# Gathering the tokens of four experts at a time, ahead of a hinted branch

## The chip, the cores and the metric

The kernel runs on one core of one Trainium2 chip. The metric is the device time of one execution, in microseconds (us); lower is better. All inputs and weights are float32.

## The reference, cut to what matters

Two transformer blocks follow each other over 256 tokens of 1024 features. The first one ends in a mixture of 16 experts. The router gives each token two experts and a weight for each. Every expert is a gated product of width 512:

```
gates = jnp.sum(jax.nn.one_hot(idx, N_EXPERTS, dtype=f32) * w[..., None], axis=1).astype(h.dtype)
out = jnp.zeros_like(ht)
for e in range(N_EXPERTS):
    hid = jax.nn.silu(ht @ w_gate[e]) * (ht @ w_up[e])
    out = out + gates[:, e:e + 1] * (hid @ w_down[e])
```

Since an expert's gate is zero for most tokens, the kernel brings only the tokens that an expert was chosen for into that expert's up to 64 places, and adds the results back to the tokens they belong to. If some expert has more than 64 tokens, a branch runs every expert over every token instead.

## The kernel before, in words

Before and after the experts the work is a stream of large products on TensorE (PE). Weights arrive by DMA from the queue of SyncE (SP) in blocks of 1 MB, in a fixed order, into a ring of buffers; a block is asked for as soon as PE has let go of an older one (`load`, line 501). VectorE (DVE) and ScalarE (ACT) move results out of PSUM. The order on every engine is the order in which the program is written down. PSUM has eight banks; four of them (`pa`) hold the experts' sum throughout, so four are left to turn over.

The experts' part goes like this, in the lines that the change touches:

- The routing (lines 1575 to 1623) makes `mask` (256 tokens by 16 experts, 0 or 1) and, by a small product on PE, `rank`, the place that a token has within each expert. The same product gives the fullest expert's count, `most`.
- `gather(g)` (line 1628) serves a pair of experts. DVE builds `dp`, a 0/1 matrix that has a one where a token stands in a place: four instructions, one for each tile of 128 tokens and each of two experts, 64 places each. PE multiplies the tokens' features by it, both halves of their float32 (`h2H`, `h2L`): for each half of the features (`kq`) sixteen matmuls with 128 columns, into one PSUM bank, which DVE copies to `xg`. Then PE turns `dp` round (`back`, the way back) and picks the gates (`gsl`).
- Of the first pair the first half is gathered ahead of the branch (`next(first)`, lines 1661 and 1678) and the second half inside the first expert (lines 1841 to 1843). The other seven pairs are gathered as side work between the products of the experts (`side.add`, `side.tick`, `side.finish`, lines 1836 to 1851).
- Each engine reads the count `most_i` into a register (line 1681) and compares (line 1682, `tc.If`). The block under it is long: it holds every expert over every token. It is jumped over in the runs here.
- `gate_up` (line 1738) multiplies an expert's places by a block of weights, two matmuls of 512 columns beside each other on the array; `hidden` turns the result, `down` (line 1762) multiplies a pair's hidden values by the second weights, `combine` (line 1787) adds them to `pa` through `back`.

Names in rows: `raw` is a block of weights, `ps` a PSUM bank, `y` the result of `down`. L379 is the helper that records all instructions of PE, DVE and ACT; L515 and L512 issue the weights (L512 those that come in two half blocks).

The pair's gather before:

```
for m in range(2):
    for a in range(2):
        e = 2 * g + a
        V.tensor_scalar(dp[:, m, a], C("slots"), rank[:, m, e:e + 1], mask[:, m, e:e + 1], op0=OP.is_equal, op1=OP.mult)
```

Of the kernel before, what the change touches and what calls it, by code (L numbers as in the profile page):

```python
# [9 lines left out]
F32 = mybir.dt.float32  # L10
F32R = mybir.dt.float32r
I32 = mybir.dt.int32
# [13 lines left out]
# ----------------------------------------------------------------------------  # L26
# Constants that depend on shapes alone
# ----------------------------------------------------------------------------
# [14 lines left out]
def shape_constants():  # L43
# [19 lines left out]
    one["slots"] = np.tile(np.arange(64)[None, :] / 16, (128, 1))  # L63
# [3 lines left out]
    # axial rotary tables over a head's columns ordered (even | odd)  # L67
# [7 lines left out]
    # forward transform over 512 points of 256 samples: real parts of bins 0..255, imaginary  # L75
    # parts of bins 1..255 with bin 256 (real) in the place of the imaginary part of bin 0
# [12 lines left out]
    # positional features of the filters  # L89
# [7 lines left out]
    # inverse frequencies of the second block's rotary embeddings  # L97
# [3 lines left out]
    # log of the number of dilated windows that hold a key, as an additive mask  # L101
# [21 lines left out]
# ----------------------------------------------------------------------------  # L123
# Layout of the inputs
# ----------------------------------------------------------------------------


def pack(w, kt, cols):
    """[K, M] -> blocks [128, kt, cols], columns outermost, then the rows' groups."""
    k, m = w.shape  # L130
    v = w.reshape(k // (128 * kt), kt, 128, m // cols, cols)
    return np.ascontiguousarray(v.transpose(3, 0, 2, 1, 4)).reshape(-1, 128, kt * cols)


def feat(v):
    """[n*128] -> [128, n]"""
    return np.ascontiguousarray(v.reshape(-1, 128).T)


def lay_out(I):  # L140
    """The inputs as the kernel reads them: moved, never changed."""
# [43 lines left out]
    # per-feature parameters, a feature per partition  # L185
# [13 lines left out]
    # small weights of the filters' network and the decay, rows on partitions  # L199
# [40 lines left out]
# ----------------------------------------------------------------------------  # L240
# Order in which the weights stream in
# ----------------------------------------------------------------------------


# queries and keys (0) and values (1) of two heads each
# [3 lines left out]
def stream_order():  # L249
    """Blocks as (name, number, groups of 128 rows, columns, cut): a block that is split into halves of  # L250
    float32 is split in pieces: two by rows' groups ("k") or by columns ("c"), three ("3"), or one ("")."""
# [69 lines left out]
# ----------------------------------------------------------------------------  # L321
# The program
# ----------------------------------------------------------------------------
# [9 lines left out]
# where the blocks of the second modulation come: branch, block of its gate or of its product  # L333
# [3 lines left out]
# quarters of a product whose operands are not split  # L337
# [3 lines left out]
class Clocked:  # L341
    """An engine whose instructions are put on a rough timeline while they are written down, so that side work
    can be told to go on when what its next products need is about to be there."""
# [39 lines left out]
class Side:  # L383
    """Work that goes on between the products of the main stream: job after job, or two beside each other."""
# [4 lines left out]
    def add(self, gen, beside=None):  # L389
        """A job that waits for the ones before it, but for the one that it goes beside."""  # L390
        self.jobs.append([gen, max(Clocked.now["S"], Clocked.now["V"]) + 0.15, beside])
        return gen

    def next(self):
        """The job that is ready first."""
        a = self.jobs[:2]
        return a[1] if len(a) > 1 and a[1][2] is a[0][0] and a[1][1] < a[0][1] else a[0]
# [12 lines left out]
    def tick(self):  # L410
        """The next job's next step, if it needn't wait."""
# [8 lines left out]
def program(ctx, tc, A, out, dump=None):  # L420
# [24 lines left out]
    def T2(shape, name):  # L445
        """Tiles for the two halves of a float32 operand, in one place if they are small."""
# [20 lines left out]
    def bcast(ap, cols):  # L467
        """A [1, cols] row in DRAM, read by every partition."""
        return bass.AP(tensor=ap.tensor, offset=ap.offset, ap=[[0, 128], [1, cols]])

    def rsqrt(v, n, tag="us"):
        """1/sqrt(v) of a [128, n] tile: a first guess from the exponent, then Newton's steps."""
# [9 lines left out]
    def rsqrt1(v, eps, n=1, between=()):  # L482
        """1/sqrt(v / n + eps) of a [128, 1] tile, the same way; other work goes between the steps."""
# [35 lines left out]
    def ahead_of(name, b):  # L519
        """How many pieces are split ahead."""  # L520
# [95 lines left out]
    def lin_feat(wh, wl, j, x, ps):  # L616
        """Features on partitions: 128 columns of the weights stay, the tokens move."""
# [6 lines left out]
    def feat_block(name, b, x, per=1):  # L624
        """A block whose pieces hold `per` groups of 128 columns: pairs of groups, a bank each."""
# [69 lines left out]
    def sin_of(dst, src, n, parts):  # L695
        """sin of any float: the argument is brought near zero first."""
# [11 lines left out]
    def hy_filters():  # L708
# [54 lines left out]
        # the spectra of the odd and the even parts, without the division by the filters' sums  # L763
# [16 lines left out]
        # the sums: a channel per partition they divide what the convolution is multiplied with, and as  # L780
        # a row they multiply the direct path that is added to the even part's first sample
# [18 lines left out]
        for o in range(2):  # L800
# [3 lines left out]
            # bin 0 has no imaginary part: bin 256 in its place  # L804
# [5 lines left out]
    # silu(c) and silu(c_ctx) in the first two of 32 columns: a product's four parts of 512 outputs  # L810
    # lie on the array's four groups of columns
# [64 lines left out]
    def modulated(s):  # L876
        """The halves of the modulated features, two groups of 128 at a time."""
# [1466 lines left out]
```

## Time and profile before

| | |
|---|---|
| time, median of 3 runs | 1444.52 us (1441.32 to 1444.76) |
| span of the profiled execution | 1439.4 us |
| PE busy | 1382.4 us, 96% of the span |
| DVE busy | 846.3 us, 59% |
| ACT busy | 629.9 us, 44% |
| TensorE clock granted, mean | 0.989 |
| moved by DMA | 297.47 MB, mean 207 GB/s |

The profiled execution has its span from the first to the last instruction; its own time is not listed beside it, but the three runs lie 1.9 to 5.4 us above the span, the median 5.1 us above. A busy engine here is one with an instruction in flight. Matmuls overlap, so PE's pace is read from the starts of successive instructions, not from the duration of one.

### The profile page before, as it was taken

How to read it: one execution, taken by the hardware profiler on the slowest of the kernel's cores; microseconds unless marked ns; L12 is line 12 of the kernel's file. 1: busy time of each engine (PE TensorE's matmuls, PEld its weight loads, DVE VectorE, ACT ScalarE, POOL GpSimd, SP SyncE). 2: the span in 40 equal slices, each digit the busy share in tenths (PEclk: the TensorE clock that was granted, in tenths of full speed). 3: DMA queues.
4: the chain of work that ended last, by engine and by line, in shares of the span. 5: the costliest groups of instructions: out<-in, count | busy, mean ns of one | idle time of the engine just before them, and what ended most of it. 6: DMA issues, size and time to landing. Idle time of an engine off the chain costs nothing.

```text
span 1439.4 us, 20751 instructions
## 1 busy us (share of the span) xinstructions
PE 1382.4 (96%) x8462; PEld 1079.5 (75%) x8462; DVE 846.3 (59%) x1555; ACT 629.9 (44%) x1012; POOL 5.8 (0%) x13
## 2 busy tenths in 40 slices
PE   6999999999999699999999899999999998999998
PEld 2678899778796344444378679999977887999996
DVE  4777457455876421121166577666585888666675
ACT  5543465644343211111147646444445664545551
POOL 0000000000000000000000000000000000000000
PEclk9999999999999899999999999999999999999999
DMA  9523444546379799999643235555444453555540
GB/s 372 211 73 114 147 175 161 209 147 229 123 247 368 282 365 391 420 421 420 240 183 118 88 107 198 194 191 211 161 162 154 145 177 125 179 202 176 207 145 30
DMA packets 44629, 297.47 MB, mean 207 GB/s; under 512 B 5186, under 2 KB 6386, under 8 KB 10288
## 3 DMA queue, kind: packets, MB, share of 16 engines
q1 hardware_dynamic: 42012, 291.02, 54.3%
q10 hardware_dynamic: 1924, 3.27, 0.7%
q0 software_dynamic: 592, 1.79, 0.5%
q8 instruction: 69, 1.13, 0.3%
q14 instruction: 32, 0.26, 0.1%
HBM read 295.00 MB, written 1.05 MB: 206 GB/s over the span
## 4 chain that ended last, share of the span: by engine, by line
PE 57%; DVE 5%; ACT 2%; DMA 1%; issue 1%; ACTq 0%; SPq 0%; DVEq 0%
PE ps L379 47%; PE pd L379 7%; DVE w L379 2%; PE pa L379 1%; PE pq L379 1%; ACT pe L379 1%; DVE v L379 1%; DMA raw<-in_ab_q 1%; DVE sm L379 1%; ACT w L379 0%; DVE rs L379 0%; PE oc L379 0%; DVE xL L379 0%; DVE rsa L379 0%; DMA pt<-in_p 0%
## 5 line engine op out<-in xcount | busy, mean ns | idle before, releaser
L379 DVE TENSOR_TENSOR w<-raw,w 128x1024 fp32r<-128x1024 f32 (+3 forms) x301 | 346.4, 1194 | 84.9 <-ACT w L379 83.8
L379 ACT ACTIVATE w<-raw 128x1024 fp32r<-128x1024 f32 (+3 forms) x301 | 293.5, 1033 | 11.1 <-DVE w L379 4.8
L379 PE MATMUL ps<-xH,w 128*128 128x256 f32 x1408 | 256.5, 283 | 0.6 <-ACT xH L379 0.6
L379 PEld LDWEIGHTS ps<-xH,w 128*128 128x128 f32 x1408 | 220.6, 192 | 1.8 <-ACT xH L379 1.1
L379 PE MATMUL ps<-xL,w 128*128 128x256 f32 x704 | 199.3, 283 | 0.7 <-DVE xL L379 0.7
L379 PE MATMUL ps<-w,xH 128*128 128x512 f32 (+2 forms) x544 | 151.3, 364 | 4.0 <-ACT xH L379 2.1
L379 PEld LDWEIGHTS ps<-xL,w 128*128 128x128 f32 x704 | 134.9, 192 | 1.8 <-DVE xL L379 1.1
L379 PE MATMUL ps<-raw,xg 128*64 128x512 f32 x512 | 121.7, 608 | 8.2 <-DVEq L1682 8.0
L379 PE MATMUL pd<-w,fh 128*128 128x512 f32 x528 | 125.6, 394 | 0.0
L379 PE MATMUL ps<-hH,w 128*128 128x256 f32 (+1 forms) x608 | 115.7, 287 | 0.0
L379 PEld LDWEIGHTS pd<-w,fh 128*128 128x128 f32 x528 | 98.3, 189 | 21.6
L379 PEld LDWEIGHTS ps<-w,xH 128*128 128x128 f32 x544 | 95.9, 190 | 19.6 <-ACT xH L379 4.0
L379 PEld LDWEIGHTS ps<-hH,w 128*128 128x128 f32 (+1 forms) x608 | 94.9, 187 | 7.9 <-issue 2.7
L379 PE MATMUL ps<-w,xL 128*128 128x512 f32 (+2 forms) x272 | 98.5, 362 | 1.9 <-DVE xL L379 1.8
L379 PE MATMUL ps<-w,hH 128*128 128x512 f32 (+1 forms) x288 | 88.1, 390 | 0.0
L379 PE MATMUL ps<-hL,w 128*128 128x256 f32 (+1 forms) x304 | 85.9, 282 | 0.0
L379 PEld LDWEIGHTS ps<-raw,xg 128*64 128x64 f32 x512 | 34.2, 139 | 66.3 <-issue 57.0
L379 DVE SCALAR_TENSOR_TENSOR fc<-ps,par,fc 128x255 f32<-128x255 f32 x88 | 42.4, 482 | 51.6 <-ACT fc L379 50.0
L379 ACT ACTIVATE fc<-ps,par 128x256 f32<-128x256 f32 x44 | 24.8, 564 | 92.3 <-PE ps L379 66.4
L379 PEld LDWEIGHTS ps<-w,hH 128*128 128x128 f32 x288 | 52.2, 188 | 13.8 <-issue 2.7
L379 PEld LDWEIGHTS ps<-w,xL 128*128 128x128 f32 x272 | 51.6, 190 | 12.0 <-DVE xL L379 5.0
L379 PE MATMUL ps<-raw,hid 128*64 128x512 f32 x256 | 57.7, 595 | 0.0
(443 smaller groups left out, 1888.5 us busy)
## 6 DMA issues: line engine op xcount, KB each, us to landing
raw<-in_moe_gu SPq DMA_DIRECT2D x62, 1024.0 KB, 9.0
raw<-in_moe_down SPq DMA_DIRECT2D x32, 1024.0 KB, 10.3
raw<-in_mod SPq DMA_DIRECT2D x24, 1024.0 KB, 4.9
raw<-in_ffn_gate SPq DMA_DIRECT2D x22, 1024.0 KB, 4.7
raw<-in_ffn_up SPq DMA_DIRECT2D x22, 1024.0 KB, 4.8
raw<-in_ffn_down SPq DMA_DIRECT2D x22, 1024.0 KB, 4.7
raw<-in_w_brg SPq DMA_DIRECT2D x12, 1024.0 KB, 5.7
raw<-in_ple_gate SPq DMA_DIRECT2D x8, 1024.0 KB, 4.7
```

The source lines that it names most:

```text
L379: return f(*args, **kw)
```

## The change

The gather now serves four experts. `dp` has the places of four (256 columns) and is built by one DVE instruction: `rank` is made one larger where a token is chosen and zero elsewhere (in one instruction that replaces the copy of `rank`), the table of places is one larger too, and a plain comparison replaces the comparison and multiplication. The matmuls have 256 columns, half as many of them; each half of the features fills two banks, and ACT copies one while DVE copies the other. `way(g)` is the part that turns `dp` round and picks the gates, still for a pair, called inside the pair's second expert. The whole first gather (both halves of the features, four experts) stands ahead of the branch; `most` and its integer are made earlier, one part of `h2L` too. A hint, `LikelyTaken`, is set for the branch on PE, DVE, ACT and SP. One block of weights fewer is asked for ahead of the branch. Two tiles used only under the branch share a buffer.

```diff
-    one["slots"] = np.tile(np.arange(64)[None, :] / 16, (128, 1))
+    one["slots"] = np.tile(np.arange(64)[None, :] / 16 + 1, (128, 1))
...
     high(1)
+    low(0, 1)
...
-    load(RAW_MOE + 2 + 2)
+    load(RAW_MOE + 2 + 1)
     rank = R(E3, "rank")
-    V.tensor_copy(rank.rearrange("p m e -> p (m e)"), ps[:, :32])
+    V.scalar_tensor_tensor(rank.rearrange("p m e -> p (m e)"), ps[:, :32], 1.0, mf, op0=OP.add, op1=OP.mult)
...
-    def gather(g):
-        dp = T([128, 2, 2, 64], "dp", F32R)
-        for m in range(2):
-            for a in range(2):
-                e = 2 * g + a
-                V.tensor_scalar(dp[:, m, a], C("slots"), rank[:, m, e:e + 1], mask[:, m, e:e + 1], op0=OP.is_equal, op1=OP.mult)
+    def gather(q):
+        dp = dps[q] = T([128, 2, 4, 64], "dp", F32R)
+        shape = [128, 2, 4, 64]
+        V.tensor_tensor(dp, rank[:, :, 4 * q:4 * q + 4].unsqueeze(3).to_broadcast(shape),
+                        C("slots").unsqueeze(1).unsqueeze(1).to_broadcast(shape), op=OP.is_equal)
         yield
-        xg = T([128, 8, 2, 64], "xg")
-        grouped[g] = xg,
-        for kq in range(2):
-            ps = PS()
+        xg = xgs[q] = [T([128, 4, 4, 64], "xg") for _ in range(2)]
+        for k4 in range(2):
+            banks = [PS(), PS()]
             for w, src in enumerate((h2H, h2L)):
-                for m in range(2):
-                    for k in range(4):
-                        c = slice((kq * 4 + k) * 128, (kq * 4 + k) * 128 + 128)
-                        P.matmul(ps[:, k * 128:k * 128 + 128], src[:, m, c], dp[:, m], start=w + m + k == 0, stop=w + m + k == 5)
-            V.tensor_copy(xg[:, kq * 4:kq * 4 + 4], ps.rearrange("p (k a s) -> p k a s", k=4, a=2))
+                for k2, ps in enumerate(banks):
+                    for m in range(2):
+                        for k in range(2):
+                            c = slice((k4 * 4 + 2 * k2 + k) * 128, (k4 * 4 + 2 * k2 + k) * 128 + 128)
+                            P.matmul(ps[:, k * 256:k * 256 + 256], src[:, m, c], dp[:, m].rearrange("p a s -> p (a s)"),
+                                     start=w + m + k == 0, stop=w + m + k == 3)
+                if w == 0 and q:
+                    yield
+            for k2, ps in enumerate(banks):
+                p4 = ps.rearrange("p (k a s) -> p k a s", k=2, a=4)
+                if k2:
+                    V.tensor_copy(xg[k4][:, 2:4], p4)
+                else:
+                    S.activation(xg[k4][:, 0:2], p4, AF.Copy)
             yield
+    def way(g):
+        d = dps[g // 2][:, :, g % 2 * 2:g % 2 * 2 + 2].rearrange("p m a s -> p m (a s)").bitcast(F32)
...
+    engines = [mybir.EngineType.PE, mybir.EngineType.DVE, mybir.EngineType.Activation, mybir.EngineType.SP]
...
     first = gather(0)
     next(first)
-    for m, n in ((0, 1), (1, 0), (1, 1)):
-        low(m, n)
+    most = R([128, 1], "most")
+    V.tensor_reduce(most, ps[:, 32:48], axis=AX, op=OP.max)
+    most_i = T([128, 1], "mosti", I32, tag="us")
+    V.tensor_scalar(most_i, most, 16.0, None, op0=OP.mult)
+    low(1, 0)
+    low(1, 1)
+    tc.mark_branch_hint_location("full", "LikelyTaken", engines=engines)
+    next(first)
+    next(first)
...
-    with tc.If(full > CAP):
+    with tc.If(full > CAP, label="full"):
...
-        if e % 2 == 0 and e + 2 < N_EXP:
-            nxt = side.add(gather(g + 1))
+        if e % 4 == 1 and e + 3 < N_EXP:
+            nxt = side.add(gather(e // 4 + 1))
...
-            if e == 0 and i == 1:
-                for _ in first:
-                    pass
             if i == 1 and e:
                 hidden(e - 1)
+            if i == 0 and e % 2:
+                way(g)
...
-        if e % 2 and e + 1 < N_EXP:
+        if e % 4 == 3 and e + 1 < N_EXP:
             side.finish(nxt)
```

Where the instructions come to stand is shown at three places. The first is the head of PE's program; `c_zt` and `pos_w` belong to the first products of the kernel.

```order
-L2331 UNCONDITIONAL_BRANCH
+L2345 UNCONDITIONAL_BRANCH
+L2345 BRANCH_PREFETCH_HINT
 L379 MATMUL ps_112<-c_zt_66,pos_w_68 64x256
 L379 MATMUL ps_132<-hid_116,pos_w_70 64x256
```

The hint stands as PE's first instruction in the program's body, more than 1,300 printed rows ahead of the branch, and not where the source marks it; on DVE, ACT and SP it stands in the same place.

The second place is DVE between the end of the routing and the branch. `h` are the normed tokens, `mod` a row of the modulation, `scores` and the rest belong to the gates.

```order
 L379 SCALAR_TENSOR_TENSOR h_4083<-h_4083,rs_4137,mod_2817 128x512
-L379 COPY rank_4235<-ps_4218 128x32
-L379 TENSOR_SCALAR dp_4237<-c_base_80,rank_4235,mask_4213 128x64 x4
 L379 TENSOR_TENSOR h2L_4091<-h_4033,h2H_4090 128x512
+L379 SCALAR_TENSOR_TENSOR rank_4232<-ps_4219,mask_4213 128x32
+L379 TENSOR_TENSOR dp_4234<-rank_4232,c_base_80 128x512
+L379 TENSOR_REDUCE most_4236<-ps_4219 128x1
+L379 TENSOR_SCALAR mosti_4238<-most_4236 128x1
 L379 TENSOR_TENSOR h2L_4091<-h_4083,h2H_4090 128x512 x2
+L379 COPY xg_4246<-ps_4249 128x512
+L379 COPY xg_4247<-ps_4269 128x512
 L379 TENSOR_SCALAR scores_4187<-scores_4187 128x32
```

The count `mosti` moved ahead of two `h2L` steps, and two copies of `xg` now stand ahead of the seven small steps on the gates, which end at the branch; before, one copy stood behind them. On PE the 32 matmuls of the first gather stand between the routing's product and the branch, where 16 stood.

The third place is PE in the experts' part, beside the second expert's weights. Before:

```order
L379 MATMUL ps_5903<-raw_4111,xg_4259 64x512 x4
L379 MATMUL ps_5959<-dp_5945,h2H_4090 128x128 x8
L379 MATMUL ps_5959<-dp_5945,h2L_4091 128x128 x8
L379 MATMUL ps_5977<-raw_4113,xg_4259 64x512 x4
L379 MATMUL ps_5984<-dp_5945,h2H_4090 128x128 x8
L379 MATMUL ps_5984<-dp_5945,h2L_4091 128x128 x8
L379 MATMUL ps_5977<-raw_4115,xg_4259 64x512 x4
```

With the change:

```order
L379 MATMUL ps_5945<-raw_4117,xg_4247 64x512 x4
L379 MATMUL ps_5987<-dp_5963,h2H_4090 128x256 x4
L379 MATMUL ps_5988<-dp_5963,h2H_4090 128x256 x4
L379 MATMUL ps_5945<-raw_4119,xg_4247 64x512 x4
L379 MATMUL ps_5987<-dp_5963,h2L_4091 128x256 x4
L379 MATMUL ps_5988<-dp_5963,h2L_4091 128x256 x4
L379 MATMUL ps_6015<-raw_4121,xg_4246 64x512 x4
```

Runs of 16 matmuls with 128 columns between blocks of weights became runs of 8 with 256 columns that fill two banks over two visits. A pair had two such runs, so four experts had four runs of 16; now they have four runs of 8. Behind the experts PE's order is the same as before.

## Rows read from the trace of the kernel before

**Rows 1.** Stretches of the span: us, busy us and instructions of each engine, clock, DMA
```profile
470.00:476.00 6.00, 3.73 (x24) 3.32 (x24) 5.22 (x21) 1.06 (x1) 0.00 (x0) 0.81 0.97 367
476.00:483.00 7.00, 0.00 (x0) 0.00 (x0) 0.71 (x2) 1.28 (x1) 0.00 (x0) 0.50 0.63 247
490.00:500.00 10.00, 9.79 (x67) 5.56 (x66) 2.65 (x9) 2.47 (x4) 0.00 (x0) 1.00 0.86 334
560.00:580.00 20.00, 20.00 (x108) 9.65 (x108) 3.12 (x8) 1.96 (x4) 0.00 (x0) 1.00 1.01 424
```
**Rows 2.** Chain that ended last, in order of time: start, us, what
```profile
533.04 2.07 PE pa L379 x8
535.11 27.15 PE ps L379 x146
```
**Rows 3.** Who waited for whom, 470 to 484 us: total, times, longest
```profile
PE ps L379 <- DVEq L1682: 8.0, 1, 8.0
```
**Rows 4.** The branch's lines: duration ns min/median/max, first and last start us
```profile
L1681 DVEq TENSOR_LOAD <-mosti x1: 541/541/541, 475.9 to 475.9; - x1
...
L1682 PEldq COMPARE_BRANCH  x1: 6187/6187/6187, 476.4 to 476.4; - x1
L1682 DVEq COMPARE_BRANCH  x1: 72/72/72, 476.5 to 476.5; - x1
...
L1682 DVEq EVENT_SEMAPHORE  x1: 21/21/21, 482.9 to 482.9; - x1
```
**Rows 5.** Timeline around the branch: start, us, engine, line, operation [idle before it <-releaser]
```profile
469.17 1.85 SPq L512 DMA_DIRECT2D raw<-in_moe_gu  x4
...
472.44 1.08 PE L379 MATMUL ps<-dp,h2H 128*128 128x128 f32 x8 [0.95 <-DVE dp L379]
...
473.36 1.75 PE L379 MATMUL ps<-dp,h2L 128*128 128x128 f32 x8
...
476.03 0.68 DVE L379 COPY xg<-ps 128x512 f32<-128x512 f32 x1
...
483.06 5.80 PE L379 MATMUL ps<-raw,xg 128*64 128x512 f32 x16 [7.95 <-DVEq L1682]
...
491.58 3.65 PE L379 MATMUL ps<-raw,xg 128*64 128x512 f32 x16 [0.21 <-DVE xg L379]
```
**Rows 6.** Timeline of one run of gather matmuls among the experts
```profile
572.01 0.97 PEld L379 LDWEIGHTS ps<-dp,h2H 128*128 128x128 f32 x8 [0.81 <-issue]
572.01 1.11 PE L379 MATMUL ps<-dp,h2H 128*128 128x128 f32 x8
...
573.94 1.94 PE L379 MATMUL ps<-raw,xg 128*64 128x512 f32 x8
```
**Rows 7.** Groups of instructions by form, 483 to 720 us
```profile
L379 PE MATMUL ps<-dp,h2H 128*128 128x128 f32 x120 | 16.6, 281 | 0.0
L379 PE MATMUL ps<-dp,h2L 128*128 128x128 f32 x120 | 15.8, 274 | 0.0
```
**Rows 8.** Timeline of PE in a later product, matmuls of 256 columns of the same type
```profile
900.00 0.28 PE L379 MATMUL ps<-xL,w 128*128 128x256 f32 x1
...
900.12 0.40 PE L379 MATMUL ps<-xH,w 128*128 128x256 f32 x2
...
900.36 0.28 PE L379 MATMUL ps<-xL,w 128*128 128x256 f32 x1
```
**Rows 9.** Last weights of the experts, their landing on the page, and their use
```profile
669.48 11.55 SPq L515 DMA_DIRECT2D raw<-in_moe_down  x4
...
raw<-in_moe_down SPq DMA_DIRECT2D x32, 1024.0 KB, 10.3
...
708.69 8.13 PE L379 MATMUL ps<-raw,hid 128*64 128x512 f32 x32
```
**Rows 10.** DMA queue that carries instructions: packets, MB, share
```profile
q8 instruction: 69, 1.13, 0.3%
```

More of the change, by code (lines that the diff above doesn't have):

```diff
@@ L1646, in gather @@
             yield
+    def way(g):
+        d = dps[g // 2][:, :, g % 2 * 2:g % 2 * 2 + 2].rearrange("p m a s -> p m (a s)").bitcast(F32)
         ps = PS()
         for m in range(2):
-            d = dp[:, m].rearrange("p a s -> p (a s)").bitcast(F32)
-            P.transpose(ps[:, m * 128:m * 128 + 128], d, ident)
+            P.transpose(ps[:, m * 128:m * 128 + 128], d[:, m], ident)
         for a in range(2):
             for m in range(2):
-                d = dp[:, m].rearrange("p a s -> p (a s)").bitcast(F32)
-                P.matmul(ps[a * 64:a * 64 + 64, 256:257], d[:, a * 64:a * 64 + 64], kept[:, m, 2 * g + a:2 * g + a + 1], start=m == 0, stop=m == 1)
+                P.matmul(ps[a * 64:a * 64 + 64, 256:257], d[:, m, a * 64:a * 64 + 64], kept[:, m, 2 * g + a:2 * g + a + 1], start=m == 0, stop=m == 1)
@@ L1657, in gather @@
         V.tensor_copy(gsl, ps[:, 256:257])
-        grouped[g] = (xg, back, gsl)
+        grouped[g] = (back, gsl)
+    engines = [mybir.EngineType.PE, mybir.EngineType.DVE, mybir.EngineType.Activation, mybir.EngineType.SP]
+    xgs, dps = {}, {}
     first = gather(0)
     next(first)
-    for m, n in ((0, 1), (1, 0), (1, 1)):
-        low(m, n)
+    most = R([128, 1], "most")
[7 more added lines that the diff above has]
+    next(first)
     V.tensor_scalar(sg, sg, 0.5, 0.5, op0=OP.mult, op1=OP.add)
@@ L1670, in program @@
     dump("gates", gates)
-    most = R([128, 1], "most")
-    V.tensor_reduce(most, ps[:, 32:48], axis=AX, op=OP.max)
-    most_i = T([128, 1], "mosti", I32, tag="us")
-    V.tensor_scalar(most_i, most, 16.0, None, op0=OP.mult)
     keep, kept = R([128, 1], "keep"), R(E3, "kept")
@@ L1677, in program @@
     V.tensor_scalar(kept, gates, keep, None, op0=OP.mult)
-    next(first)
     full = nc.values_load(most_i[0:1, 0:1], min_val=0, max_val=N)
-    with tc.If(full > CAP):
+    with tc.If(full > CAP, label="full"):
         fT = [h2s[m] for m in range(2)]
@@ L1685, in program @@
         gu = {(q, m): PS("full") for q in range(2) for m in range(2)}
-        hfs, hts = ([T([128, 512], "full") for _ in range(2)] for _ in range(2))
+        hfs, hts = (lambda t: (t[:, 0], t[:, 1]))(T([128, 2, 512], "full")), [T([128, 512], "full") for _ in range(2)]
         turn = [0]
@@ L1741, in gate_up @@
         for k in range(2):
-            x = grouped[e // 2][0][:, 2 * i + k, e % 2]
+            x = xgs[e // 4][i // 2][:, (2 * i + k) % 4, e % 4]
             for a, q in enumerate((low, high)):
@@ L1762, in down @@
     def down(g):
-        _, back, gsl = grouped.pop(g)
+        back, gsl = grouped.pop(g)
         hid = hids.pop(g)
```

## The prediction

> **What bounds the kernel now.** I read the stretches first, then the chain, the waits and the timeline. The stretches show that among the experts PE is never idle and holds its full clock, while DVE works 3.1 of 20 us and ACT 2.0 [rows 1]. The chain is PE alone there: 2.07 us in `pa` and 27.15 us in `ps`, 29.22 us for each pair of experts [rows 2]. So every PE microsecond taken out of a pair shortens the kernel, as long as the weights keep up. DMA moves 424 GB/s in that stretch and is full [rows 1], so this must be asked below. The other place is the branch. From 476 to 483 us PE does nothing [rows 1]; its first expert product waits 8.0 us, and what releases it last is DVE's sequencer at the branch [rows 3]. PE's own compare-and-branch takes 6.19 us; DVE's compare at 476.5 is followed by its next event at 482.9 [rows 4]. Nothing in these rows computes: both engines jump over a long block and wait for instructions.
>
> **Term 1: the gathers behind the branch.** Before, 240 matmuls stand there [rows 7], 15 runs of 16. One run, from 572.01 to the next product at 573.94, takes 1.93 us [rows 6]; 15 x 1.93 = 29.0 us. Eight weight loads of 0.19 us each fill 0.97 us, so loads follow each other every 0.11 us: (0.97 - 0.19) / 7. A run is thus 16 x 0.11 = 1.78 us and about 0.15 us of change-over. With the change 96 matmuls of 256 columns remain, in 12 runs of 8. Three such matmuls of the same type start within 900.00 to 900.36, 0.12 us each [rows 8]. Twice the columns cost 0.01 us more, because the narrow ones did not run at the pace of their columns. A new run is 8 x 0.12 + 0.15 = 1.11 us, 12 of them 13.3 us. I take **-15.7 us**. Without a change-over the new ones cost 11.5 us (-17.5), with a double one 15.1 us (-13.9).
>
> [...]
>
> **Term 2: when the experts start.** Ahead of the branch work is added. `h2L` now goes ahead of `rank` on DVE, while `dp` is one instruction of 512 elements, about the 0.68 us of a 512-element copy [rows 5]. I let PE start its gather near 472.7 instead of 472.44. It then has 32 matmuls: 3.8 us at full clock, so 476.5 at best. The clock was halved before PE stopped: the mean of 0.81 over 470 to 476 means 2.3 us at half, from 473.7 [rows 1], and eight `h2L` matmuls took 1.75 us [rows 5]. If it falls again at the same moment, some 24 matmuls take twice 0.12 us and the gather ends at 479.5. A copy of 0.68 us follows. So `xg` is ready between 477.2 and 480.2, and PE can start the experts there at the earliest. DVE, whose passing of the branch PE waits for, reaches it later than before: its sequencer runs ahead of its copies (its read of the count began at 475.9, ahead of the copy at 476.03 [rows 4, 5]), but two copies and seven steps now stand in front. I put its branch between 478 and 481.5.
>
> If the hint works, the 6.2 us after the compare go, the first product starts between 478 and 482, and I take 480.3, in the middle: 483.06 - 480.3 gives **-2.8 us** (-5 to -1). Nothing in the trace shows a hinted branch, so the ends are no stall and the whole stall of rows 4. If it does not work, DVE pays its fetch from about 480: with the full 6.4 us of before the start is at 486.4. It may be shorter, since before the last weights were issued until 471 and DMA still moved 247 GB/s in the stall [rows 1, 5], while now one block fewer is in flight and it is older; 3.3 us is my lower end, so 483.3. The middle is 484.8, 1.7 us later than before.
>
> **Term 3: the clock after the branch.** The first sixteen expert matmuls took 5.80 us, the same sixteen at 491.58 took 3.65 [rows 5]: 2.15 us lost, since PE had been idle. With a shorter pause some of that comes back; I take half, **-1.1 us** (0 to -2.15) with a working hint, and nothing without.
>
> **What costs nothing.** The eight extra ACT copies of about 0.7 us lie beside PE, as do the DVE copies; both engines are mostly idle there [rows 1]. `way` issues per pair what the old gather issued per pair. One block of weights fewer ahead of the branch is covered by 18 blocks on hand, some 40 us of PE work. Do the weights then keep up? Each pair needs 12 blocks of 1.049 MB; at 424 GB/s that is 29.7 us, and PE will ask for them every 27.3. The last block was issued at 680.7, landed 10.3 us later at about 691, and was used in the second half of the row that starts at 708.69, near 712.8 [rows 9]: 21.8 us early. My forecast eats some 19 of these if no weight comes sooner. But SP asks when PE lets go, so the first requests after the branch come 2.8 us sooner, and until 560 us DMA has room (334 GB/s from 490 to 500 [rows 1]). About 10 us of cover should be left. If it were gone, PE would fall back to 29.7 us a pair, next to the old pace.
>
> **The sum.** -15.7 - 2.8 - 1.1 = -19.6 us on the profiled span of 1439.4: 1419.8. The median of the runs lies 5.1 us above that span, so the forecast is **1424.9 us**. What follows the experts has the same order and moves as a whole.
>
> **Rivals.** (1) *The hint does nothing.* It stands at the head of the program [the first place shown], 475 us ahead of the branch, and the instruction queue brings 69 blocks over the span [rows 10], so about a third of them come in between. [...] For: that placement. [...] Then -15.7 + 1.7 = -14.0: **1430.5 us**. [...]
>
> (2) *PSUM replaces the matmuls as the bound.* Four banks turn over, and a gather now holds two of them across a block of weights, while `gate_up`, `hidden` and `down` want one or two each. If each of the 12 runs waited for one copy of 0.68 us, 8 us would go back: about 1424.9 + 8 = **1433 us**. Against: at least one block of weights (1.9 us, rows 6) stands between a bank's last matmul and its next use in the order shown.
>
> [...]
>
> **Chances.** The forecast 0.62, rival 1 0.28, rival 2 0.07, rival 3 0.03. Around the forecast the ends of the terms give -24.7 to -14.9, so 1420 to 1430; rival 1 spans -17.5 + 0.2 to -13.9 + 3.3, so 1427 to 1434. Adding a run's scatter of some 2 us, 1418 to 1435 holds all but the outer part of rival 2, rival 3 and both terms at their ends. A measurement of this kernel tells 0.3%, 4.3 us, from no change. The first three cases are all faster by more, but for a small part of rival 2: faster 0.95, within 0.3% 0.02, slower 0.03.
>
> **What would show it.** Right: 96 gather matmuls of 256 columns behind the branch at 0.12 us; 27.3 us on average per pair of experts in the chain, without waits for `raw`; PE's compare-and-branch far under 6 us, and the first expert product near 480 us. Rival 1 would show the long compare-and-branch or DVE's next event some 3 to 6 us behind its compare. Rival 2 would show PE idle ahead of gather matmuls, released by `xg` copies. [...] I am wrong if matmuls of this gather take 0.2 us each, or if PE waits for landings of `raw` from about 600 us on.

## The result, and the profile after

The changed kernel takes 1423.3 us (median of four runs, 1420.1 to 1433.0) against 1443.3 us beside it. The ratio is 0.9877 with a 95% interval of 0.9841 to 0.9913, so it is faster by 1.2%. The profiled execution took 1420.13 us and its span is 1418.4 us, 21.0 us less than before. The forecast was 1424.9 us and a span of 1419.8 us. Each execution takes 1.7 to 1.8 us more than its span.

Where the 21.0 us lie is read from four marks in PE's timeline: the first matmul with `mask` (the routing's sums), the first expert product, the end of the last product with `hid`, and the end of the span.

| stretch, us | before | after | difference |
|---|---|---|---|
| start to the first `mask` matmul | 470.43 | 469.74 | -0.69 |
| from there to the first expert product | 12.64 | 11.04 | -1.60 |
| from there to the end of the last `hid` product | 233.75 | 216.39 | -17.36 |
| from there to the end | 722.6 | 721.2 | -1.4 |

The first and the last row are work that the change does not touch. They hold 2.1 of the 21.0 us. Behind the experts the execution before stands at half clock once more than the one after (3.4 us from 750.2 us on); what made the first row shorter is not shown.

The stretches after, in the columns of [rows 1]:

```profile
470.00:476.00 6.00, 4.88 (x32) 4.81 (x32) 3.87 (x9) 1.65 (x2) 0.00 (x0) 0.77 0.99 380
476.00:483.00 7.00, 3.70 (x16) 2.13 (x16) 3.61 (x19) 2.31 (x4) 0.00 (x0) 0.74 0.12 45
490.00:500.00 10.00, 10.00 (x62) 4.45 (x58) 1.18 (x3) 3.06 (x5) 0.00 (x0) 1.00 1.01 422
560.00:580.00 20.00, 20.00 (x103) 7.93 (x102) 4.40 (x8) 3.49 (x7) 0.00 (x0) 1.00 1.02 423
```

From 476 to 483 PE now works 3.70 us where it worked none [rows 1], and its mean clock is 0.74 instead of 0.50. Among the experts PE is still never idle. DMA is full from 490 us on, not only later.

The chain that ended last, among the experts, in the columns of [rows 2]:

```profile
525.94 22.98 PE ps L379 x114
548.93 2.07 PE pa L379 x8
551.00 27.83 PE ps L379 x146
578.82 2.07 PE pa L379 x8
```

Before, each pair of experts took 29.22 us [rows 2]. Now pairs alternate: 22.98 + 2.07 = 25.05 us without a gather, 27.83 + 2.07 = 29.90 us with one. Four experts take 54.95 us, a pair 27.5 us on average. No wait for `raw` stands in the chain.

The branch's line, in the columns of [rows 4]:

```profile
L1697 PEldq COMPARE_BRANCH  x1: 392/392/392, 474.6 to 474.6; - x1
...
L1697 DVEq COMPARE_BRANCH  x1: 84/84/84, 479.9 to 479.9; - x1
L1697 DVEq EVENT_SEMAPHORE  x1: 21/21/21, 480.5 to 480.5; - x1
```

PE's compare-and-branch takes 0.39 us instead of 6.19, and DVE's next event follows its compare by 0.6 us instead of 6.4 [rows 4]. PE's sequencer passes the branch at 474.6, while its gather matmuls are still running; DVE is the last, 5.3 us later.

The timeline around the branch, as in [rows 5]:

```profile
471.93 1.19 PE L379 MATMUL ps<-dp,h2H 128*128 128x256 f32 x8 [1.12 <-DVE most L379]
...
474.38 1.91 PE L379 MATMUL ps<-dp,h2H 128*128 128x256 f32 x8
...
476.08 1.39 PE L379 MATMUL ps<-dp,h2L 128*128 128x256 f32 x8
...
477.51 0.69 DVE L379 COPY xg<-ps 128x512 f32<-128x512 f32 x1 [2.21 <-PE ps L379]
478.12 0.17 DVE L379 TENSOR_SCALAR scores<-scores 128x32 f32<-128x32 f32 x1
...
479.26 0.24 DVE L379 TENSOR_SCALAR kept<-gates,keep 128x32 f32<-128x32 f32 x1
...
480.78 10.15 PE L379 MATMUL ps<-raw,xg 128*64 128x512 f32 x40 [3.30 <-DVE posf L379]
```

The gather is done on PE at 477.47 and copied at 478.20. Then DVE makes seven small steps until 479.50, and only behind them comes its branch. The first expert product starts at 480.78, 3.27 us behind the start of DVE's last copy. What is left of the wait, 3.30 us, is DVE's.

One gather run among the experts, as in [rows 6]:

```profile
495.79 1.21 PE L379 MATMUL ps<-dp,h2H 128*128 128x256 f32 x8
...
496.94 1.94 PE L379 MATMUL ps<-raw,xg 128*64 128x512 f32 x8
```

A run of eight wide matmuls takes 1.15 us to the next product, where a run of 16 narrow ones took 1.93 [rows 6].

### The profile page after: what moved, and what is told of

Same layout as the page of the kernel before. It is cut to its first block, busy times and chain, and to the rows that moved or that the text cites. A ratio compares the mean times of both kernels' runs of the same rounds, so it can differ in the third digit from the quotient of the medians.

```text
span 1418.4 us, 20472 instructions
## 1 busy us (share of the span) xinstructions
PE 1365.9 (96%) x8334; PEld 1065.1 (75%) x8334; DVE 836.1 (59%) x1519; ACT 634.6 (45%) x1020; POOL 5.8 (0%) x13
## 3 DMA queue, kind: packets, MB, share of 16 engines
q10 hardware_dynamic: 1924, 3.27, 0.7%
## 4 chain that ended last, share of the span: by engine, by line
PE 56%; DVE 5%; ACT 2%; DMA 1%; issue 1%; ACTq 0%; SPq 0%; DVEq 0%
PE ps L379 47%; PE pd L379 7%; DVE w L379 2%; PE pa L379 1%; PE pq L379 1%; ACT pe L379 1%; DVE v L379 1%; DMA raw<-in_ab_q 1%; DVE sm L379 1%; ACT w L379 0%; DVE rs L379 0%; PE oc L379 0%; DVE xL L379 0%; DVE rsa L379 0%; DMA pt<-in_p 0%
## 5 line engine op out<-in xcount | busy, mean ns | idle before, releaser
L379 PEld LDWEIGHTS ps<-hL,w 128*128 128x128 f32 (+1 forms) x304 | 56.9, 187 | 0.6
## 6 DMA issues: line engine op xcount, KB each, us to landing
raw<-in_moe_down SPq DMA_DIRECT2D x32, 1024.0 KB, 11.3
```

The lines of the kernel that those rows point to most:

```text
L379: return f(*args, **kw)
```

## The experiments

Each experiment has a profile, from which the two middle stretches of the table above are taken, with the mean granted clock of the first, and the median of its runs. The kernel before ran beside them: 1444.1 us beside e0 to e3, 1444.6 beside e4 to e7, 1442.5 beside e8 to e11. These are all twelve, and the two kernels that the study compares:

| kernel | mask to experts, us | clock there | experts to last `hid`, us | median, us (ratio to before, 95%) |
|---|---|---|---|---|
| before | 12.64 | 0.63 | 233.75 | 1443.3 |
| the change | 11.04 | 0.82 | 216.39 | 1423.3 (0.9877, 0.9841 to 0.9913) |
| e0_again, the change | 12.01 | 0.67 | 217.85 | 1425.8 (0.9863, 0.9834 to 0.9892) |
| e1_no_hint | 14.58 | 0.66 | 216.87 | 1426.9 (0.9881, 0.9851 to 0.9910) |
| e2_hint_only | 7.37 | 0.54 | 233.31 | 1437.4 (0.9946, 0.9927 to 0.9965) |
| e3_narrow | 9.65 | 1.00 | 226.17 | 1435.7 (0.9926, 0.9900 to 0.9952) |
| e4_gates_early | 10.35 | 0.67 | 215.04 | 1422.0 (0.9839, 0.9818 to 0.9859) |
| e5_half_behind | 7.49 | 0.58 | 219.22 | 1422.7 (0.9849, 0.9830 to 0.9868) |
| e6_no_dve_hint | 13.10 | 0.83 | 217.85 | 1428.3 (0.9886, 0.9869 to 0.9903) |
| e7_no_pe_hint | 12.02 | 0.67 | 217.92 | 1427.7 (0.9867, 0.9843 to 0.9891) |
| e8_before_less | 10.98 | 0.54 | 233.31 | 1439.5 (0.9985, 0.9971 to 0.9998) |
| e10_after_base, the change | 10.99 | 0.84 | 216.74 | 1426.5 (0.9879, 0.9852 to 0.9906) |
| e11_gates_early2 | 10.26 | 0.67 | 215.04 | 1418.9 (0.9841, 0.9823 to 0.9859) |
| e9_count_early | 9.79 | 0.65 | 215.18 | 1420.5 (0.9842, 0.9828 to 0.9856) |

The stretches separate what the medians cannot: runs of the changed kernel spread over 13 us with their mean granted clock (see the last section). The stretches move with the clock too, but by less. The changed kernel's first stretch took 11.0 and 12.0 us; in e3, whose program is the same up to the branch, it took 9.65 us, all at full clock. So first stretches are compared at about the same clock. The second moves by 1.5 us in the changed kernel.

### The base once more

The changed kernel without any edit.

> The changed kernel once more, as the base of these comparisons. Its runs lay between 1420 and 1433 us, the longer ones at a lower mean granted clock. If that belongs to this kernel, several of six runs again lie over 1425 us at a clock below 0.99, and the kernel before beside it stays within 1441 to 1445 us; if it was chance of those runs, all lie within 1420 to 1424 us.

Its six runs lie between 1420.8 and 1432.9 us, four of them over 1425 us, and the clock falls from 0.992 in the shortest to 0.981 in the longest. So the scatter was no chance of the first four runs. The second half of the expectation failed: the scatter is not this kernel's alone, for the kernel before does not stay within 1441 to 1445 us either. Its 17 runs reach from 1440.6 to 1450.2 us at 0.989 to 0.980.

### The hint taken out

```
-    tc.mark_branch_hint_location("full", "LikelyTaken", engines=engines)
```

> The changed kernel without the branch hint, all else as it is. Theory (the hint takes the stall out, and DVE, the last engine at the branch, carries it): DVE's compare stays near 479.9 and its next event comes 3.3 to 6.4 us later instead of 0.6 us, PE's compare-and-branch goes back from 0.4 us to several us, the first expert product moves from 480.8 to 483.5-486.5, and the kernel takes 1426 to 1430 us against 1423. Rival (the short branch comes from the earlier weights' end and from PE's sequencer running ahead of its matmuls, not from the hint): first product still within 0.5 us of 480.8, 1423 us.

The branch's line without the hint:

```profile
L1696 PEldq COMPARE_BRANCH  x1: 3747/3747/3747, 476.3 to 476.3; - x1
...
L1696 DVEq COMPARE_BRANCH  x1: 72/72/72, 481.6 to 481.6; - x1
L1696 DVEq EVENT_SEMAPHORE  x1: 21/21/21, 484.7 to 484.7; - x1
```

DVE's event comes 3.1 us behind its compare instead of 0.6, just under the 3.3 expected, and PE's compare-and-branch takes 3.7 us instead of 0.39. The first stretch is 14.58 us, 2.6 us longer than with the hint at about the same clock (12.01 in e0_again). The median rises by only 1.1 us, which the runs' scatter hides; at the same mean clock, 0.992, the two shortest runs are 1424.4 and 1424.9 us against 1420.1 and 1420.8 with the hint. So the hint works, and in this kernel DVE's share of it is worth 2.5 us at the branch. The rival, that the branch became short by itself, falls. But the stall without the hint is 3.1 us here and was 6.4 in the kernel before: half of it had gone for another reason, which an experiment below looks for.

### The hint alone

```
+    tc.mark_branch_hint_location("full", "LikelyTaken", engines=engines)
...
-    with tc.If(full > CAP):
+    with tc.If(full > CAP, label="full"):
```

These lines are put into the kernel before.

> The kernel before with the hint added and nothing else. Theory: PE's compare-and-branch falls from 6.2 us to about 0.4, DVE's next event follows its compare by 0.6 us, the first expert product moves from 483.1 to 477.2-477.8, and with up to 1 us of clock the kernel gains 5 to 7 us: about 1437 us, a ratio of 0.995 to 0.9965. Rival (the hint is worth nothing at this distance): no change, 1443 us, first product at 483.

The branch's line in this kernel:

```profile
L1684 PEldq COMPARE_BRANCH  x1: 397/397/397, 481.6 to 481.6; - x1
...
L1684 DVEq COMPARE_BRANCH  x1: 84/84/84, 482.0 to 482.0; - x1
...
L1684 DVEq EVENT_SEMAPHORE  x1: 21/21/21, 482.6 to 482.6; - x1
```

PE's 6.19 us become 0.40, DVE's 6.4 us become 0.6, and the first stretch falls from 12.64 to 7.37 us, by 5.3. (This execution came to the branch some 5 us later, for the whole start-up did; the stretch is free of that.) The median falls by 6.7 us, ratio 0.9946, about a third of what the whole change takes off the median. Beside the changed kernel's first stretch, 7.37 says something else: **the wider first gather, all of it ahead of the branch, costs 2.3 to 4.6 us of what the hint gives**, by the clock in its stretch (9.65 us in e3, 11.04 in the first profile of the change, 12.01 in e0_again). The order on DVE has a part in this, measured below.

### The wide matmuls undone

```
-                            P.matmul(ps[:, k * 256:k * 256 + 256], src[:, m, c], dp[:, m].rearrange("p a s -> p (a s)"),
-                                     start=w + m + k == 0, stop=w + m + k == 3)
+                            d = dp[:, m].rearrange("p a s -> p (a s)")
+                            for z in range(2) if q else (None,):
+                                o, x = (k * 256, d) if z is None else (k * 256 + z * 128, d[:, z * 128:z * 128 + 128])
+                                P.matmul(ps[:, o:o + x.shape[1]], src[:, m, c], x,
+                                         start=w + m + k == 0 and not z, stop=w + m + k == 3 and z != 0)
```

> The changed kernel with each 256-column gather matmul behind the branch issued as two of 128 columns: the same columns and the same 12 runs, 192 matmuls instead of 96. Theory (a narrow matmul of this type costs 0.11 us, nearly as much as a wide one): each run grows from 1.15 to about 1.93 us, 12 x 0.78 = 9.4 us, a pair of experts costs 28.3 us on average, about 1432.5 us. Rival (matmuls cost by columns): 0 to 1 us, 1423 to 1424 us. Second rival (part of the gain is hidden by weights that come late): less than 5 us, with PE waiting for raw in both.

The same run of the gather as narrow matmuls, in the timeline:

```profile
500.36 2.00 PE L379 MATMUL ps<-dp,h2H 128*128 128x128 f32 x16
502.29 1.94 PE L379 MATMUL ps<-raw,xg 128*64 128x512 f32 x8
```

A run is back at 1.93 us, the second stretch is 9.8 us longer than the change's (226.17 against 216.39), and the median is 9.9 us above the base beside it. Summed over the rows, from each matmul's start to the next one's, the 192 narrow matmuls take 22.97 us, 0.12 us each, and the 96 wide ones 13.55 us, 0.14 us each, change-over included. The same columns in half as many matmuls are 9.4 us cheaper, as expected. The rival by which matmuls cost by their columns falls, and so does the one by which late weights hide part of the gain.

How far this goes can be read from other products of the same type in the trace of the kernel before, each matmul with a weight load of its own. The median from one start to the next is 0.112 us with the gather's 128 columns, 0.120 with 256, 0.175 with 384 and about 0.23 with 512. So here, from 128 to 256 columns, the number of matmuls decides, and from there to 512 the columns do. What sets the 0.112 us is not shown; that the weight load does is the author's estimate, from sixteen matmuls with only 16 columns, though of plain float32, which start every 0.112 us as well:

```profile
464.07 1.98 PE L379 MATMUL ps<-par,h2T 128*128 128x16 f32 x16
```

### Which engine's hint counts

```
-    engines = [mybir.EngineType.PE, mybir.EngineType.DVE, mybir.EngineType.Activation, mybir.EngineType.SP]
+    engines = [mybir.EngineType.PE, mybir.EngineType.Activation, mybir.EngineType.SP]
```

> The changed kernel with the hint for PE, ACT and SP but not for DVE. Theory (DVE's share of the hint is the one that counts, since DVE comes last): PE's compare-and-branch stays at 0.4 us, DVE's event comes 3.1 us behind its compare as without any hint, and the stretch from mask product to first expert product is 13.5 to 14.6 us, as without the hint. Rival (PE's share counts): 11 to 12 us.

DVE at the branch, without its share of the hint:

```profile
L1697 DVEq COMPARE_BRANCH  x1: 72/72/72, 480.5 to 480.5; - x1
L1697 DVEq EVENT_SEMAPHORE  x1: 21/21/21, 483.4 to 483.4; - x1
```

The other list leaves PE out instead of DVE:

> The changed kernel with the hint for DVE, ACT and SP but not for PE. Theory (PE's sequencer runs ahead of its matmuls and takes its stall while they still run): PE's compare-and-branch is 3 to 4 us long but begins some 5 us ahead of DVE's event, so the stretch from mask product to first expert product stays at 11 to 12 us. Rival (PE's share counts): 13.5 us or more.

The branch's line there:

```profile
L1697 PEldq COMPARE_BRANCH  x1: 3487/3487/3487, 476.4 to 476.4; - x1
...
L1697 DVEq EVENT_SEMAPHORE  x1: 21/21/21, 482.0 to 482.0; - x1
```

Without DVE's hint its event comes 2.9 us behind its compare, and the first stretch is 13.10 us; the expectation's lower end was 13.5, and this execution ran most of its gather at full clock. At about that clock the changed kernel took 11.0 us, 2.1 us less. Without PE's hint PE stalls 3.5 us, from 476.4 to 479.9, but DVE's event comes at 482.0 anyway, and the stretch is 12.02 us, as with the whole hint at that clock. Of these two shares, then, only that of DVE, the last engine at the branch, counts in this kernel. ACT's and SP's shares were not taken out alone.

### DVE's queue at the branch

The seven gate steps are written ahead of the copies:

```
+    V.tensor_scalar(sg, sg, 0.5, 0.5, op0=OP.mult, op1=OP.add)
...
+    V.tensor_scalar(kept, gates, keep, None, op0=OP.mult)
     next(first)
     next(first)
-    V.tensor_scalar(sg, sg, 0.5, 0.5, op0=OP.mult, op1=OP.add)
...
-    V.tensor_scalar(kept, gates, keep, None, op0=OP.mult)
```

> The changed kernel with the seven small gate steps of DVE (scores to kept) written ahead of the two xg copies of the first gather, so that they run while DVE waits for PE. Theory (DVE is the last engine at the branch and its queue sets the start): DVE's compare comes some 1.4 us sooner behind the last xg copy, the stretch from the first mask product to the first expert product falls from 11.0 (12.0 where the clock is lower) to about 9.6 (10.6) us, the kernel gains 1.4 us, about 0.1%, which the runs hardly tell. Rival (ACT or PE is the one that sets it): stretch unchanged.

And the same kernel again, beside the changed kernel:

> The changed kernel, as the base of the two beside it: 11.0 to 12.0 us from mask product to first expert product, 216.4 to 217.9 us from there to the last product with hid, median 1423 to 1426 us.

> The version with the early gate steps again, now beside the changed kernel on one chip. If its gain is real: 9.6 to 10.4 us and 215.0 to 216.5 us in the two stretches, and a median 1.5 to 3.5 us below the changed kernel's. If the lower times were chance of the clock: the same median within 1 us, and the sum of the two stretches again at 227 us or more.

The timeline of the second of these executions:

```profile
475.29 0.24 DVE L379 TENSOR_SCALAR kept<-gates,keep 128x32 f32<-128x32 f32 x1
...
479.16 0.69 DVE L379 COPY xg<-ps 128x512 f32<-128x512 f32 x1 [1.78 <-PE ps L379]
...
480.68 8.80 PE L379 MATMUL ps<-raw,xg 128*64 128x512 f32 x40 [1.55 <-DVE posf L379]
```

The steps now end at 475.53, while DVE waits for PE anyway. From the start of DVE's last copy to the first expert product it is 1.52 us instead of 3.27 (1.58 in the first execution, and 3.27 again in the base beside it): 1.75 us gained there. The first stretch is 10.35 and 10.26 us although both executions ran three of the four gather runs at half clock, where the changed kernel needed 12.0. Both stretches together take 225.3 us, the change's 227.7 in the execution beside it: 2.4 us. Most of this, 1.7 us, lies in the second stretch, where the programs are the same: the first 16 expert products take 3.45 us at full clock here and 5.15 us, part of them at half, in the base. They ran at full clock in all three executions with the early steps and the whole gather ahead; that the steps are the cause is not shown. The medians differ by 7.6 us, more than the stretches explain; the rest goes with the clock (0.989 to 0.995 here, 0.981 to 0.993 there). The intervals of the two ratios overlap, so by the runs alone the gain is not shown; the 1.75 us at the branch are, by the rows.

One step further, the engines read the count ahead of the last copies:

```
     next(first)
+    full = nc.values_load(most_i[0:1, 0:1], min_val=0, max_val=N)
     next(first)
-    full = nc.values_load(most_i[0:1, 0:1], min_val=0, max_val=N)
```

> The version with the early gate steps, and the engines' read of the count written ahead of the last two xg copies (the compare stays behind them). Theory (DVE's read, 0.54 us, lies between the start of its last copy and its compare): compare and first expert product come 0.3 to 0.6 us sooner, the first stretch is 9.8 us where the early gate steps alone give 10.35. Rival (the copy itself then sets the start): less than 0.2 us.

The timeline from DVE's last copy to the first expert product:

```profile
479.18 0.69 DVE L379 COPY xg<-ps 128x512 f32<-128x512 f32 x1 [2.12 <-PE ps L379]
...
480.19 8.80 PE L379 MATMUL ps<-raw,xg 128*64 128x512 f32 x40 [1.04 <-DVE posf L379]
```

1.01 us from copy to product, 0.5 less again, and the first stretch is 9.79 us. With 225.0 us this has the shortest sum of both stretches in the study. The runs do not tell it from the early steps alone: the median is 1420.5 against 1418.9 us.

### Half of the first gather behind the branch

```
+            if e == 0 and i == 0:
+                for _ in first:
+                    pass
```

Only one `next(first)` stays ahead of the branch, with the gate steps early.

> As the kernel with the early gate steps, and the second half of the first gather stands behind the branch, after the first expert's first block. Theory: DVE reaches the branch about 3 us sooner, the stretch from the mask product to the first expert product falls to about 7 us, while the stretch from there to the last product with hid grows by the moved half, 2.0 to 2.5 us, from 216.4 to about 218.7; together 225.7 against 227.4 us, a gain of 1.5 to 2 us on the changed kernel. Rival: the moved half waits for its copy before the third block, and what the branch gains is lost again: sum 227 to 229 us.

7.49 us and 219.22 us, 226.7 us together. Against the change's 227.4 and 227.7 us this is a gain of about 1 us, less than the 1.5 to 2 expected, and worse than the early steps with the gather whole (225.4 and 225.3); the medians, 1422.7 and 1422.0 us, do not tell the two apart. The timeline of PE shows why:

```profile
477.96 3.68 PE L379 MATMUL ps<-raw,xg 128*64 128x512 f32 x8 [1.55 <-DVE posf L379]
481.57 1.35 PE L379 MATMUL ps<-dp,h2H 128*128 128x256 f32 x8
482.76 1.12 PE L379 MATMUL ps<-dp,h2L 128*128 128x256 f32 x8
483.81 2.41 PE L379 MATMUL ps<-raw,xg 128*64 128x512 f32 x10
```

The moved half does not wait for its copy, so the rival falls; its two runs take 2.24 us. But the first eight expert products need 3.61 us to the next matmul, at half clock, where the early gate steps alone have them in 1.74 us, from 480.68 on, at full clock. The granted clock was halved from 471.6 to 481.9 us here, and from 471.0 to 477.8 us in the second execution of the early steps. There it had risen before the gather was done; with half the gather ahead it had not, and the first expert products were slow.

### Why the stall without a hint was halved

```
-    load(RAW_MOE + 2 + 2)
+    load(RAW_MOE + 2 + 1)
```

This edit is made in the kernel before: the ring of weights is filled one block less far ahead of the branch, as the change does.

> The kernel before with one block of weights (2 of 4 half requests) fewer asked for ahead of the branch, without a hint. Theory (an unhinted branch waits for instructions that queue behind the weights: 249 GB/s moved in the 6.4 us of before, 3 GB/s in the 3.1 us of the changed kernel without hint): DVE's event follows its compare by 4 to 5 us instead of 6.4, as about 2.5 us of weights fewer lie in front, and the stretch from mask product to first expert product falls from 12.6 to 10.5-11 us. Rival (the stall is a matter of the code that is jumped to): 6.4 us stay, 12.6 us.

The branch's line in this kernel, with no hint:

```profile
L1682 PEldq COMPARE_BRANCH  x1: 4547/4547/4547, 481.6 to 481.6; - x1
...
L1682 DVEq COMPARE_BRANCH  x1: 72/72/72, 481.9 to 481.9; - x1
...
L1682 DVEq EVENT_SEMAPHORE  x1: 21/21/21, 484.9 to 484.9; - x1
```

DVE's stall is 3.0 us, below the 4 to 5 expected, PE's 4.5 us, and PE is now the last. The first stretch is 10.98 us, within what the theory said. The median falls by 3.0 us; the ratio of 0.9985 (interval 0.9971 to 0.9998) says 2.2 us, and the two stretches 2.1. What DMA moved during DVE's stall is in the last column of the stretches. The kernel before:

```profile
476.50:482.90 6.40, 0.00 (x0) 0.00 (x0) 0.21 (x1) 1.28 (x1) 0.00 (x0) 0.50 0.62 249
```

This kernel, with one block fewer under way:

```profile
481.90:484.90 3.00, 0.00 (x0) 0.00 (x0) 0.10 (x1) 1.28 (x1) 0.00 (x0) 0.50 0.22 79
```

The changed kernel without its hint:

```profile
481.60:484.70 3.10, 0.00 (x0) 0.00 (x0) 0.00 (x0) 0.00 (x0) 0.00 (x0) 0.54 0.01 3
```

With 249 GB/s of weights in the same moments the stall is 6.4 us, with 79 GB/s 3.0, with 3 GB/s 3.1. So about 3 us is what the unhinted branch costs DVE here by itself, and with the weights of the kernel before on their way it is 6.4. PE's goes from 6.2 to 4.5 us.

The rows of the DMA queues (packets, MB, share, as in [rows 10]) show where the time goes. In the kernel before, from PE's compare at 476.4 until 480.0 us, only the queue that brings the weights moves anything:

```profile
q1 hardware_dynamic: 404, 1.48, 100.9%
```

The first packets of the queues that carry instructions come between 480.0 and the end of the stall at 482.9 us, when the weights are nearly done:

```profile
q1 hardware_dynamic: 39, 0.10, 9.6%
q14 instruction: 3, 0.02, 2.2%
q8 instruction: 1, 0.02, 2.1%
```

They start 3.6 us behind DVE's compare. With one block fewer under way the first starts 0.7 us behind it, at 482.6. The hinted branch did not feel the weights: with the hint alone they moved 418 GB/s from PE's compare at 481.6 to DVE's event at 482.6 us, DVE's event came 0.6 us behind its compare all the same, and no instruction packet stands in that stretch:

```profile
q1 hardware_dynamic: 115, 0.42, 102.1%
```

So no instructions were brought while the hinted engines passed the branch. When theirs had come is not shown.

## Why the prediction was right

The forecast's span was 1.4 us above the measured one, and its mechanism stands in the profile as described. That the number came so near is in part luck: 2.1 of the 21.0 us lie outside the two stretches that the change touches and were no part of the forecast. The 5.1 us from span to median held by luck as well. Only 1.7 to 1.8 us of them belong to an execution; the rest is that the profiled execution was among the shortest both times (1441.2 us by this step, and 1420.1). By its own terms:

- **Gathers behind the branch, forecast -15.7 us.** From start to start, 240 narrow matmuls took 28.9 us and the 96 wide ones take 13.55: -15.3. The forecast of a run was 1.11 us, it is 1.15. Undoing the width alone gives 9.4 us back, so of the 15.3 us some 9.4 are the width and 5.9 the three runs that went ahead of the branch, at the price of narrow matmuls.
- **Start of the experts, forecast -2.8 us, to 480.3.** It came at 480.78: -2.3 us, of which 0.7 lie ahead of the routing, so the change itself gave 1.6. DVE's branch was forecast between 478 and 481.5 and came at 479.9; it is DVE that sets the start, as argued, and the clock did fall in the gather (half from 473.3 to 476.7). What the forecast priced only inside that bracket are DVE's seven steps behind the copy. Writing them sooner is worth 1.75 us.
- **Start without a working hint, forecast 483.3 to 486.4, middle 484.8.** The changed kernel without the hint: 14.58 us behind the `mask` matmul, which is 484.3 on the profile's time. The lower end of the stall was taken as 3.3 us because one block fewer is under way; it measured 3.1, just below, and the kernel before with that block fewer measured 3.0. This argument held. The whole price of a hint without effect was too high: 5.6 us lie between the forecast and rival 1, while the two stretches together are 1.6 us (e0_again) to 4.0 us (the first profile) longer without the hint, and the median is 1426.9 us, where rival 1 stood at 1430.5.
- **Clock behind the branch, forecast -1.1 us.** From the first start to the next product's start, the first 16 expert products take 4.82 us, with the full clock 3.45 (the early gate steps): 1.37 us lost where the forecast read 2.15 us before, so -0.8. In e0_again they take 6.28 us, and nothing of this term is left. That PE's pause sets the clock, as the prediction has it, is not shown: in the kernel before the clock stood at half from 473.8 us, while PE still worked, to 487.4; with the change it was full from 476.7 to 480.1, where PE worked only 0.78 of 3.40 us, and half from 480.1 to 483.5.
- **What costs nothing.** Six of the eight ACT copies stand behind the branch, and PE waits for none of them. About 10 us of cover were forecast for the weights. The rows that answer to [rows 9]:

```profile
654.93 15.21 SPq L515 DMA_DIRECT2D raw<-in_moe_down  x4
...
raw<-in_moe_down SPq DMA_DIRECT2D x32, 1024.0 KB, 11.3
...
689.07 8.10 PE L379 MATMUL ps<-raw,hid 128*64 128x512 f32 x32
```

The last request is made at 669.8, a third of a microsecond before its row ends. With the 11.3 us of the median it lands near 681.1, and it is used in the second half of the last row, near 693.1: 12.0 us early. DMA moves about 420 GB/s from 490 to 680 us, so this cover would go on shrinking if PE got faster still.

The sum of the terms as measured: -15.3 - 2.3 - 0.8 = -18.4 us; the remaining 2.6 us are the 1.4 us behind the experts, which no part of the change touches, and some 1 us among them: the products with `kept`, `pa` and `hid` and the later expert products each take a few tenths less.

Of the rivals, the idle hint (1) falls by the two experiments on it. Its place at the head of the program did not keep it from working: some 475 us later PE's compare-and-branch takes 0.39 us with it, 3.7 us without (e1). Where DVE had no hint, its event came 2.9 to 6.4 us behind its compare, and in the kernel before four packets of instructions start in that stall (above). That the weights in flight lengthen it is read from e8: 6.4 us with 249 GB/s, 3.0 us with 79. PSUM as the bound (2) does not show: among the experts PE waits once, 0.7 us for ACT's `gu`, and it did so before (0.8 us). Harm from the hint (3) does not show either: the hint alone makes the kernel faster (ratio 0.9946), and in the changed kernel the queue that carries instructions brings 67 packets where it brought 69 [rows 10].

Not undone alone were the single instruction that builds `dp`, the copies shared between ACT and DVE and the earlier count, so their shares of the gain are not known.

## What to carry to other kernels

Between 128 and 256 moving columns, each matmul with a weight load of its own, a row of matmuls cost by their number here (0.112 us from start to start with 128, 0.120 with 256): join what shares the stationary operand before anything else. The branch taken over a long block held DVE, without a hint, for about 3 us by itself and for 6.4 us behind weights that DMA was moving at 249 GB/s; with the hint it was 0.6 us. So hint such a branch, or keep the queue empty around it; then see which engine comes last, and take out of that engine's queue everything that could run sooner. And work put ahead of a branch is not free because an engine was idle there. With the hint, the gather moved there costs 2.3 to 4.6 us ahead of the branch. Behind it, it would cost 5.9 us as narrow matmuls, but only about 3.4 us as wide ones (three runs of 1.13 us), so whether the move by itself pays is not shown. With half of it moved back (e5) both stretches took 1.3 us more, with the first expert products at half clock.

## What had not been expected

That the unhinted stall depends on the weights in flight (above) had been a lower end of a range, not a forecast.

The hint and the other part overlap: alone the hint takes 5.3 us off the first stretch, in the changed kernel 2.6 us at the same clock. The change asks for one block less ahead of the branch, and that alone takes DVE's stall from 6.4 to 3.0 us (e8).

The changed kernel's runs scatter with the clock far from the change. Over 16 runs it took 1420.1 to 1433.3 us; the 15 runs of the versions with the early gate steps and the whole first gather ahead of the branch took 1417.0 to 1424.1. In the base that took 1432.9 us, a stretch at the start and two long after the experts stand at half clock (two of the three are shown):

```profile
28.80:39.00 10.20, 10.20 (x28) 3.09 (x24) 5.53 (x8) 3.28 (x3) 0.94 (x1) 0.50 1.02 423
813.90:820.70 6.80, 5.98 (x26) 4.65 (x27) 2.50 (x13) 1.47 (x3) 0.00 (x0) 0.50 0.01 2
```

and the same times in the execution that took 1420.1 us do not:

```profile
28.80:39.00 10.20, 10.18 (x56) 3.29 (x52) 9.15 (x10) 3.83 (x2) 0.94 (x1) 1.00 1.01 417
813.90:820.70 6.80, 6.80 (x44) 5.19 (x41) 5.22 (x12) 6.14 (x15) 0.00 (x0) 1.00 0.37 116
```

The spans differ by 12.7 us. The first `mask` matmul came at 475.3 us there and at 469.7 us here, 5.6 us for the same instructions, and what follows the experts took 725.9 us there and 721.2 us here, 4.7 us. Why some executions get these dips stays open. The early steps do not keep them all away: their first execution has four behind the experts. Whether they keep some away, or 15 runs only happened to miss the longest, stays open too.
